# Moving token operands and weights of a hybrid decoder layer to eight different relative places within 512 bytes

## The chip, the cores and the metric

The kernel runs on one core of one Trainium2 chip. The metric is the device time of one execution in microseconds (us). A core has a matrix engine (TensorE, PE in the profile, with its weight loads as PEld), a vector engine (DVE), a scalar engine (ACT), GpSimd (POOL) and SyncE (SP), which here issues most DMAs. Operands of a matmul lie in SBUF, a memory of 128 partitions; a tile takes the same bytes in each partition, and "place" here means the byte address of a tile within a partition.

## The reference

One layer of a decoder on 512 tokens of width 2048, all in float32:

```
h = rmsnorm(x, attn_pre_norm)
proj = h @ w_in                      # 2048 x 6160: q, k, v, gate of 4 GLA heads,
                                     # 16 columns for the forget gate, q, k, v of 4 diff heads
o_a = rmsnorm(gla_chunked(q, k, v, log_sigmoid(ga @ w_alpha_up + b_alpha) / 16)) * silu(gate)
o_b = rmsnorm(diff_attention(q, k, v, lam)) * (1 - lambda_init)
x = x + rmsnorm(concat(o_a, o_b) @ w_o, attn_post_norm)
h = rmsnorm(x, ffn_pre_norm)
a, b = split(h @ w_ffn_in)           # 2048 x 11264, two branches of 5632
a = causal depthwise conv of width 3 over the tokens, with bias
f = (gelu(a) * b) @ w_ffn_out        # 5632 x 2048
x = x + rmsnorm(f, ffn_post_norm)
```

## The kernel before, in words

**Products in three parts.** Each float32 operand of a large product is held as a high part rounded to the matmul's own format (float32r) and a low part, the rest. A product is three matmuls into the same PSUM bank: high by high, and the two cross products. `split` (L127, L128) makes the parts of token operands: ACT writes the high part, DVE the low one by subtraction. `granule` (L104 to L117) does the same to a loaded piece of weights of 128 x 1024: `raw` becomes `whi` (L114, ACT) and `wlo` (L115, DVE), three buffers each; where a spare pool is given, the pieces are called `xhi` and `xlo`.

**Token operands.** `ah` and `al` hold the high and the low part of all 512 tokens by 2048 features, as 4 token blocks by 16 feature blocks of 128 x 128. They are rewritten three times: normed input, mixer output, input of the FFN, and in the down projection they hold the sums of the hidden values.

**Order.** The mixer's input projections come first: `proj_t` (products at L150 to L152: weights stationary, 512 tokens streamed) and `proj_n` (L168 to L170: tokens stationary, 512 weight columns streamed). Attention and gated linear attention are generators whose steps are filled in between projection steps. The forget gate (L364, L365) has its own small stationary weights, a tile `gas` of 16 groups of 80 columns in the pool `mx`. The output projection follows with the FFN's first pieces (`to_ffn`, an order written out by hand). All other stages are ordered by the planner, which simulates the engines and lets each instruction go where its operands and buffers would be ready.

**The FFN in units.** After a first group of 512 hidden columns the up projection runs in 20 units (10 groups by two branches). A unit computes a 2 x 2 block product with seven instead of eight block products (Strassen and Winograd's scheme), so it needs sums of token blocks: `s5`, `s2`, `s3` (and `s7`, which overwrites a block of `ah`, `al`). These sums are made once by `up_sums`, each as a high and a low tile of 8 KB per partition: `s5h`, `s5l`, `s2h`, `s2l`, `s3h`, `s3l`, in the pool `fa`. The products are L897 to L899: a 128 x 128 weight block is stationary, 256 token columns are streamed. `Unit.run` takes the segments in the order `a11`, `s5`, `s2`, `s3`, `a12`, `s7`, `a22`. POOL and SP load and add weight blocks.

At the end of each second unit `token_sums` makes four sums of the hidden values on DVE (L965), `s5`, `s2`, `s7`, `s3` in that order, each in a tile of tag `sum` with four buffers, and each is stored to DRAM by a DMA on SP's queue. `s2` reads `s5`, `s3` reads `s2`. The down projection (L994 to L996) runs in 10 units with the tokens stationary and 512 weight columns streamed, and reads the stored sums back.

**Where tiles lie.** Pools are stacked in the order in which they are opened; within a pool tiles follow each other. A pool that is closed gives its room to the next. Left to right: `pad` (128 bytes), `ah`, `al` (32768 bytes each), the pool `w` (`raw`, `whi`, `wlo`, 4096 bytes each), then the mixer's pools, of which the first (`mx1`) holds a tile `masks` of 1792 bytes; after the mixer the pool `wo` of the output projection; and after that `rp` (four `rt` of 4096 bytes) and `fa` (the six sums, six `u`, two `p1`, four `sum`). `masks` is the only tile among the matmul operands' pools whose length, modulo 512, isn't 0. `fa` ends where the pools on the right side begin, to the byte.

Of the kernel before, what the change touches and what calls it, by code (L numbers as in the profile page):

```python
# [9 lines left out]
F32 = mybir.dt.float32  # L10
F32R = mybir.dt.float32r
# [6 lines left out]
P = 128  # L18
# [17 lines left out]
def hybrid_layer(ctx: ExitStack, tc: tile.TileContext, x, attn_pre_norm, w_in, w_alpha_up, b_alpha,  # L36
# [3 lines left out]
    nc = tc.nc  # L40
# [6 lines left out]
    def dma(o, i):  # L47
        return nc.sync.dma_start(out=o, in_=i)
# [9 lines left out]
    const = ctx.enter_context(tc.tile_pool(name="const", bufs=1))  # L58
# [9 lines left out]
    nc.vector.memset(nhalf, -0.5)  # L68


    pad = const.tile([P, 32], F32, name="pad")
    nc.vector.memset(pad, 0.0)
    ah = const.tile([P, NT, KT, P], F32R, name="ah")
    al = const.tile([P, NT, KT, P], F32R, name="al")
    wpool = ctx.enter_context(tc.tile_pool(name="w", bufs=3))

    def bank(pool=None):
# [653 lines left out]
    fp = fa.enter_context(tc.tile_pool(name="fa", bufs=2))  # L731
# [43 lines left out]
    HK = KT // 2  # L775
    part = {"a11": (0, 0), "a12": (0, 1), "s7": (1, 0), "a22": (1, 1)}
    up = {}
    for n, (i, j) in part.items():
        up[n] = tuple(v[:, 2 * i:2 * i + 2, HK * j:HK * (j + 1), :] for v in (ah, al))
    for n in ("s5", "s2", "s3"):  # L780
        up[n] = tuple(fp.tile([P, 2, HK, P], F32R, name=f"{n}{v}", bufs=1) for v in "hl")
    s7raw = []

    def up_sums():
# [170 lines left out]
    def token_sums(gi, u0, u1):  # L955
        c, i = (gi - 1) // 2, (gi - 1) % 2
        T = [slice(0, 256), slice(256, 512)]
        a11, a21, a12, a22 = u0[:, :, T[0]], u0[:, :, T[1]], u1[:, :, T[0]], u1[:, :, T[1]]

        def put(n, src):  # L960
            dma(sd[c][n][:, i, :].rearrange("p (n t) -> p n t", n=2), src)

        def add(n, x, y, op):
            t = fp.tile([P, 2, 256], F32, name=n, tag="sum", bufs=4)
            tt(t, x, y, op)  # L965
            put(n, t)
            return t

        put("a11", a11)
        put("a12", a12)  # L970
        put("a22", a22)
        s5 = add("s5", a21, a22, ALU.subtract)
        s2 = add("s2", s5, a11, ALU.subtract)
        add("s7", a11, a21, ALU.subtract)
        add("s3", s2, a12, ALU.add)
# [219 lines left out]
```

## Time and profile before

| | |
|---|---|
| median of 3 runs | 2190.66 us (2188.64 to 2194.54) |
| profiled execution | 2189.8 us |
| its span, first to last instruction | 2188.1 us |
| mean granted TensorE clock | 0.996 |
| instructions | 31879, of which 13009 matmuls and as many weight loads |

Lines of groups read: line of the kernel, engine, operation, written tile <- read tiles, shapes, count, then busy time in us and mean ns of one, then idle time of the engine just before and what ended it. Lines of the timeline read: start in us, duration in us, engine, line, operation. The duration of a matmul reaches from its start to the end of its last column's way through the array and overlaps the next one's; the distance between starts is what a matmul costs in a dense stretch.

### The profile page before, as it was taken

The numbers are of one execution on the slowest core, as the hardware profiler recorded it, in microseconds if no ns is written. First come the engines' busy times: TensorE is split into PE (matmuls) and PEld (weight loads), VectorE is DVE, ScalarE is ACT, GpSimd is POOL, SyncE is SP. The second block draws the span as 40 slices with busy tenths as digits, with TensorE's granted clock in tenths as the row PEclk, the third lists the DMA queues.
The fourth block names the chain that finished last, engine by engine and source line by source line (L and its number), as shares of the span: only waits on it lengthen the run. The fifth ranks groups of instructions, "written<-read, shape, count | busy, mean of one in ns | idle before, by whom it ended". The sixth has DMA issues, their size and how long they took to land.

```text
span 2188.1 us, 31879 instructions
## 1 busy us (share of the span) xinstructions
PE 2152.7 (98%) x13009; PEld 1921.7 (88%) x13009; DVE 1418.9 (65%) x1722; ACT 901.2 (41%) x1162; POOL 204.6 (9%) x245
## 2 busy tenths in 40 slices
PE   7999999999999999999999999999999999999997
PEld 6878888888888889899999999999999878787886
DVE  5345554444453245886786776776777777888987
ACT  4233332333342233453443444444444464544433
POOL 1000000000000000011111111011011011011101
PEclk9999999999999999999999999999999999999999
DMA  6322222223224344447657667567567678677663
GB/s 210 103 68 79 76 78 77 78 77 87 78 87 166 104 154 154 124 109 179 154 126 183 145 136 181 138 150 175 134 157 178 173 212 218 173 187 184 151 175 136
DMA packets 218471, 303.83 MB, mean 139 GB/s; under 512 B 11776, under 2 KB 155572, under 8 KB 216404
## 3 DMA queue, kind: packets, MB, share of 16 engines
q1 hardware_dynamic: 165204, 238.87, 32.4%
q0 software_dynamic: 53120, 62.92, 18.5%
q8 instruction: 102, 1.67, 0.3%
q14 instruction: 45, 0.37, 0.0%
HBM read 273.97 MB, written 27.79 MB: 138 GB/s over the span
## 4 chain that ended last, share of the span: by engine, by line
issue 50%; PE 42%; POOL 4%; DVE 2%; DMA 1%; ACT 1%; POOLq 0%; SPq 0%; DVEq 0%; ACTq 0%
PE bank L168 7%; PE bank L169 7%; PE bank L170 7%; PE bank L152 5%; PE bank L150 5%; PE bank L151 4%; POOL rt L846 2%; POOL raw L846 2%; PE bank L417 1%; PE bank L995 1%; PE bank L996 1%; PE bank L994 1%; PE bank L485 1%; PE bank L516 1%; PE bank L135 1%
## 5 line engine op out<-in xcount | busy, mean ns | idle before, releaser
L115 DVE TENSOR_TENSOR wlo<-raw,whi 128x1024 fp32r<-128x1024 f32 x307 | 374.7, 1223 | 357.8 <-ACT whi L114 346.7
L114 ACT ACTIVATE whi<-raw 128x1024 fp32r<-128x1024 f32 x307 | 324.6, 1058 | 604.7 <-PE bank L898 185.6
L899 PE MATMUL bank<-ah,wlo 128*128 128x256 f32 x1280 | 362.9, 284 | 0.0
L898 PE MATMUL bank<-al,whi 128*128 128x256 f32 x1280 | 362.9, 284 | 0.0
L897 PE MATMUL bank<-ah,whi 128*128 128x256 f32 x1280 | 362.9, 284 | 0.0
L115 DVE TENSOR_TENSOR wlo<-rt,whi 128x1024 fp32r<-128x1024 f32 x220 | 268.1, 1222 | 114.9 <-ACT whi L114 114.6
L114 ACT ACTIVATE whi<-rt 128x1024 fp32r<-128x1024 f32 x220 | 232.1, 1058 | 260.9 <-PE bank L898 201.3
L897 PEld LDWEIGHTS bank<-ah,whi 128*128 128x128 f32 x1280 | 246.3, 192 | 0.1
L898 PEld LDWEIGHTS bank<-al,whi 128*128 128x128 f32 x1280 | 246.2, 192 | 0.1
L899 PEld LDWEIGHTS bank<-ah,wlo 128*128 128x128 f32 x1280 | 246.2, 192 | 0.0
L168 PE MATMUL bank<-whi,ah 128*128 128x512 f32 x600 | 237.5, 399 | 0.8 <-ACT ah L127 0.8
L169 PE MATMUL bank<-wlo,ah 128*128 128x512 f32 x600 | 236.3, 394 | 0.0
L170 PE MATMUL bank<-whi,al 128*128 128x512 f32 x600 | 235.5, 394 | 0.0
L150 PE MATMUL bank<-ah,whi 128*128 128x512 f32 (+1 forms) x512 | 196.4, 384 | 0.0
L152 PE MATMUL bank<-ah,wlo 128*128 128x512 f32 (+1 forms) x512 | 194.9, 381 | 0.0
L151 PE MATMUL bank<-al,whi 128*128 128x512 f32 (+1 forms) x512 | 194.8, 380 | 0.0
L995 PE MATMUL bank<-wlo,ah 128*128 128x512 f32 x420 | 164.1, 391 | 2.2 <-DVE wlo L115 2.2
L996 PE MATMUL bank<-whi,al 128*128 128x512 f32 x420 | 163.6, 390 | 0.0
L994 PE MATMUL bank<-whi,ah 128*128 128x512 f32 x420 | 156.4, 391 | 0.6 <-DVE acc L1002 0.6
L170 PEld LDWEIGHTS bank<-whi,al 128*128 128x128 f32 x600 | 113.4, 189 | 24.3 <-DVE al L128 0.3
L168 PEld LDWEIGHTS bank<-whi,ah 128*128 128x128 f32 x600 | 113.4, 189 | 24.1 <-ACT ah L127 1.2
L169 PEld LDWEIGHTS bank<-wlo,ah 128*128 128x128 f32 x600 | 113.5, 189 | 23.6 <-DVE wlo L115 0.5
(251 smaller groups left out, 4110.9 us busy)
## 6 DMA issues: line engine op xcount, KB each, us to landing
raw<-in_w_in_dram SPq DMA_DIRECT2D x96, 512.0 KB, 3.7
raw<-in_w_ffn_in_dram SPq DMA_DIRECT2D x96, 512.0 KB, 4.7
raw<-in_w_ffn_out_dram SPq DMA_DIRECT2D x48, 512.0 KB, 6.3
rt<-in_w_ffn_in_dram SPq DMA_DIRECT2D x40, 512.0 KB, 5.6
rt<-in_w_ffn_in_dram POOLq DMA_DIRECT2D x40, 512.0 KB, 5.9
raw<-in_w_ffn_in_dram POOLq DMA_DIRECT2D x40, 512.0 KB, 7.0
raw<-in_w_o_dram SPq DMA_DIRECT2D x32, 512.0 KB, 3.7
rt<-in_w_ffn_out_dram SPq DMA_DIRECT2D x20, 512.0 KB, 6.9
```

Source lines behind the costliest of these rows:

```text
L114: act(hi, raw, AF.Copy)
L115: tt(lo, raw, hi.bitcast(F32), ALU.subtract)
L150: mm(o, wh, ah[:, t0:t1, kk, :], start=st, stop=False)
L151: mm(o, wh, al[:, t0:t1, kk, :], start=False, stop=False)
L152: mm(o, wl, ah[:, t0:t1, kk, :], start=False, stop=sp)
L168: mm(banks[t], ah[:, t, s, :], w[0][:, k, :], start=st, stop=False)
L169: mm(banks[t], ah[:, t, s, :], w[1][:, k, :], start=False, stop=False)
L170: mm(banks[t], al[:, t, s, :], w[0][:, k, :], start=False, stop=sp)
L897: mm(o, wh, sh[:, :, kk, :], start=start and kk == 0 and n == 0, stop=False, **NOW)
L898: mm(o, wh, sl[:, :, kk, :], start=False, stop=False, **NOW)
L899: mm(o, wl, sh[:, :, kk, :], start=False, stop=kk == HK - 1, **NOW)
L995: mm(b[j], sh[:, o:o + P], w[1][:, q, :], start=False, stop=False, **NOW)
```

## The change

Nine small tiles that only take room ("rooms") are put between tiles that matmuls read, each filled once with zeros by DVE. Before and behind `al` stand rooms of 32 words (128 bytes), so that `ah`, `al` and the weight pool lie 128 bytes apart within 512 bytes; `room0` is the former `pad`. In the pool `fa` the six high and low tiles of the sums are allocated in another order, each behind a room of 8 to 48 words. The sums of the hidden values get three buffers in place of four, which makes the space for the rooms: `s3` then takes the buffer of `s5`. No matmul, conversion or DMA is added or removed.

Counted from the start of the weight pool within 512 bytes, the token tiles lie, after the change: `ah` at 256, `al` at 384, `s2l` at 192, `s2h` at 320, `s3l` at 352, `s5l` at 416, `s5h` at 480, `s3h` at 32. Before it all lie at 0. In the pool `wo` and in the pool of the down stage, which hold no rooms, spare weights lie as those of `w` do, before and after.

```diff
-    pad = const.tile([P, 32], F32, name="pad")
-    nc.vector.memset(pad, 0.0)
+    def room(pool, name, words):
+        nc.vector.memset(pool.tile([P, words], F32, name=name, bufs=1), 0.0)
+
+    room(const, "room0", 32)
     ah = const.tile([P, NT, KT, P], F32R, name="ah")
+    room(const, "room1", 32)
     al = const.tile([P, NT, KT, P], F32R, name="al")
+    room(const, "room2", 32)
     wpool = ctx.enter_context(tc.tile_pool(name="w", bufs=3))
...
+    late = {}
+    for n, words in (("s2l", 48), ("s2h", 32), ("s3l", 8), ("s5l", 16), ("s5h", 16), ("s3h", 16)):
+        room(fp, f"room{n}", words)
+        late[n] = fp.tile([P, 2, HK, P], F32R, name=n, bufs=1)
     for n in ("s5", "s2", "s3"):
-        up[n] = tuple(fp.tile([P, 2, HK, P], F32R, name=f"{n}{v}", bufs=1) for v in "hl")
+        up[n] = (late[n + "h"], late[n + "l"])
...
         def add(n, x, y, op):
-            t = fp.tile([P, 2, 256], F32, name=n, tag="sum", bufs=4)
+            t = fp.tile([P, 2, 256], F32, name=n, tag="sum", bufs=3)
             tt(t, x, y, op)
```

## The prediction

> **What bounds the kernel now.** I read the page's busy shares and its slices first, then the table of windows, then PE's timeline, then the weight loads and who waits for whom.
>
> ```profile
> PE 2152.7 (98%) x13009; PEld 1921.7 (88%) x13009; DVE 1418.9 (65%) x1722; ACT 901.2 (41%) x1162; POOL 204.6 (9%) x245
> PE   7999999999999999999999999999999999999997
> PEclk9999999999999999999999999999999999999999
> ```
>
> TensorE is busy in 98% of the span, in every slice but the first and the last at 90% or more, and its clock is granted throughout. So the time is the number of matmuls times the distance between their starts. That distance is what the change can touch, and it has to be read from starts, since the durations in the page overlap.
>
> ```profile
> 75.00:380.00 305.00, 305.00 (x1474) 254.86 (x1474) 147.38 (x243) 98.42 (x148) 16.65 (x32) 1.00 0.26 78
> 932.00:1740.00 808.00, 808.00 (x6713) 806.88 (x6711) 594.45 (x601) 372.74 (x405) 102.49 (x80) 1.00 0.65 154
> ```
>
> Columns: the stretch, its length, then busy time and count of PE, PEld, DVE, ACT, POOL, clock, DMA share, GB/s. The second stretch is the up projection by units: 808.00 us over 6713 matmuls of 256 columns are 120.4 ns each, with weight loads going on nearly all the time (806.88 us) and no hole in PE. In the first stretch PE has no hole either. The long matmuls stand in the timeline; here are the first and the last of 58 in a row (57 distances):
>
> ```profile
> 492.45 0.39 PE L152 MATMUL bank<-ah,wlo 128*128 128x512 f32 x1
> ...
> 505.37 0.39 PE L152 MATMUL bank<-ah,wlo 128*128 128x512 f32 x1
> ```
>
> (505.37 - 492.45) / 57 = 226.7 ns for 512 columns. From 256 to 512 columns the distance grows by 106.3 ns, so 226.7 is twice that plus 14, and 120.4 is that plus 14: each matmul carries some 14 ns beside its columns, in both shapes. A part of it comes from the weight load that runs beside it:
>
> ```profile
> 844.27 0.19 PEld L150 LDWEIGHTS bank<-ah,xhi 128*128 128x128 f32 x1
> 844.39 0.19 PEld L151 LDWEIGHTS bank<-al,xhi 128*128 128x128 f32 x1
> 845.14 0.19 PEld L152 LDWEIGHTS bank<-ah,xlo 128*128 128x128 f32 x1 [0.55 <-DVE xlo L115]
> 845.25 0.19 PEld L150 LDWEIGHTS bank<-ah,xhi 128*128 128x128 f32 x1
> 845.37 0.19 PEld L151 LDWEIGHTS bank<-al,xhi 128*128 128x128 f32 x1
> ```
>
> Beside a running matmul loads start 0.12 us apart (844.27 to 844.39, and 845.25 to 845.37). After the wait, with no matmul streaming, the next load starts 0.11 us later (845.14 to 845.25). So about 10 ns of the 120 go with the reading of weights and of the streamed operand at the same time. In before all these operands lie at the same place within 512 bytes: every tile between `ah` and the `fa` pool is a multiple of 512 bytes long.
>
> **The change, part by part.** *Places.* After the change the weights lie, counted from the token operand within 512 bytes, at 256 (`ah`), 128 (`al`), 320 (`s2l`), 192 (`s2h`), 160 (`s3l`), 96 (`s5l`), 32 (`s5h`), 480 (`s3h`); in before at 0 for all. Where tokens are the stationary operand (output projections, down units) 256 stays and 128 turns into 384. What runs beside matmul n is the weight load of matmul n+1, so one triple (high by high, and the two cross products) has two pairs at the relation of its high part and one at that of its low part. No instruction is added to TensorE. The counts, from the groups with shapes kept apart (the three products of a triple have equal counts):
>
> ```profile
> L899 PE MATMUL bank<-ah,wlo 128*128 128x256 f32 x1280 | 362.9, 284 | 0.0
> L168 PE MATMUL bank<-whi,ah 128*128 128x512 f32 x600 | 237.5, 399 | 0.8 <-ACT ah L127 0.8
> L150 PE MATMUL bank<-ah,whi 128*128 128x512 f32 x448 | 178.2, 398 | 0.0
> L995 PE MATMUL bank<-wlo,ah 128*128 128x512 f32 x420 | 164.1, 391 | 2.2 <-DVE wlo L115 2.2
> L899 PE MATMUL bank<-s3h,wlo 128*128 128x256 f32 x320 | 90.7, 284 | 0.0
> L995 PE MATMUL bank<-xlo,ah 128*128 128x512 f32 x140 | 55.9, 399 | 0.6 <-DVE xlo L115 0.4
> L1102 PE MATMUL bank<-wlo,ah 128*128 128x512 f32 x56 | 21.9, 391 | 0.2 <-DVE wlo L115 0.2
> ```
>
> What does another relation cost? Before has two places that show one. The first granule of spare weights in the opening stage (`xhi`, `xlo` of pool `mx`) lies 256 from `ah` and `al`, since `masks` is 1792 bytes long:
>
> ```profile
> 51.85 0.40 PE L169 MATMUL bank<-xlo,ah 128*128 128x512 f32 x1
> 52.09 0.39 PE L170 MATMUL bank<-xhi,al 128*128 128x512 f32 x1
> 52.32 0.39 PE L168 MATMUL bank<-xhi,ah 128*128 128x512 f32 x1
> ...
> 52.99 0.39 PE L170 MATMUL bank<-whi,al 128*128 128x512 f32 x1
> ```
>
> After two slow ones behind the transposes (0.24, 0.23), three distances take 0.67 us, 223 ns each with the rounding of the rows, which is not above the 226.7. So relation 256 costs nothing, and that covers all pairs whose high part is `ah`. The other place is the forget gate, whose weights `gas` advance by 320 bytes per step, and so pass through 256, 64, 384, 192, 0, 320, 128 and 448 while `ah` and `al` stream:
>
> ```profile
> 124.47 0.40 PE L364 MATMUL bank<-ah,gas 128*80 128x512 f32 x1
> 124.71 0.39 PE L365 MATMUL bank<-al,gas 128*80 128x512 f32 x1
> 124.94 0.39 PE L364 MATMUL bank<-ah,gas 128*80 128x512 f32 x1
> 125.17 0.39 PE L365 MATMUL bank<-al,gas 128*80 128x512 f32 x1
> ...
> 131.58 0.39 PE L365 MATMUL bank<-al,gas 128*80 128x512 f32 x1
> 131.81 0.39 PE L168 MATMUL bank<-whi,ah 128*128 128x512 f32 x1
> ```
>
> 32 distances take 131.81 - 124.47 = 7.34 us, 229.4 ns each, 2.7 ns above the 226.7 at relation 0; the largest is 0.24 us, about 13 ns above. These loads have 80 columns rather than 128, and their relation changes every second matmul, as the relation in the changed kernel does within each triple. I take the mean, +2.7 ns, for each pair at a relation other than 0 and 256, in both shapes, because the 14 ns were the same in both:
>
> - 512 columns: the rows give 600 + 448 + 420 + 140 + 56 = 1664 triples, one pair each at 128 or 384: 1664 x 2.7 ns = 4.5 us.
> - 256 columns on `ah`/`al`: 1280 x 2.7 ns = 3.5 us.
> - 256 columns on the six late tiles: 3 operands x 3 products x 320 = 2880 matmuls, all moved: 2880 x 2.7 ns = 7.8 us.
>
> Together 15.8 us, all of it on the path, since PE has no holes there. Both ends of the price: below, the 10 ns of the load beside a matmul vanish for the moved pairs of 256 columns, (1280 + 2880) x 10 ns = -42 us (the long ones have the load in the first half of the stream, where I see no gain). Above, every moved pair costs the gate's largest, (1664 + 1280 + 2880) x 13 ns = +76 us. The mean lies between them and comes from the nearest rows, so I take it.
>
> *The rooms.* Nine fills on DVE in place of one, by the one that is there:
>
> ```profile
> L72 DVE MEMSET pad<- 128x32 f32 x1 | 0.1, 85 | 0.0
> PE bank L168 <- ACT ah L127: 0.8, 1, 0.8
> PE bank L995 <- DVE wlo L115: 2.2, 5, 0.5
> ```
>
> 85 ns each: 8 x 0.085 = 0.7 us. Two more at the start lie where DVE waits for the first inputs. The six late ones go over memory that the output projection used, so DVE has to wait until its last reader, PE on the spare weights among them, is done, and the conversions of the next weights queue behind. Three weight buffers cover that; the longest that PE waits for a converted `wlo` in the whole run is 0.5 us. I cost it at nothing, and if that cover is gone, at a few us once: 0 to +5. A gain isn't possible, as nothing is taken away.
>
> *One buffer fewer for the sums.* `s3` now takes the buffer of `s5`, whose store must have landed:
>
> ```profile
> 1020.13 0.69 DVE L965 TENSOR_TENSOR s<-u 128x512 f32<-128x512 f32 x1
> ...
> 1025.94 0.69 DVE L965 TENSOR_TENSOR s<-s,u 128x512 f32<-128x512 f32 x1
> 1020.85 6.13 SPq L48 DMA_DIRECT2D sd0s<-s  x4
> sd3s<-s SPq DMA_DIRECT2D x8, 256.0 KB, 3.8
> ```
>
> `s5` ends at 1020.82 and its store is issued at 1020.85 on SP's queue; the slowest group of these stores takes 3.8 us in the median, so it lands near 1024.7, and `s3` starts at 1025.94: 1.2 us to spare. Should a store be late by 2 us, DVE would stand still with the next `wlo` behind it, ten times in the run. DVE is busy 594 of 808 us there and has holes to make it up, so 0, at most 10 x 2 = +20 us if PE had to wait each time. The planner may also order DVE's work a little differently; with PE's waits as small as above I take 0.
>
> **The sum.** The profiled execution took 2189.8 us (span 2188.1 and 1.7 around it). 2189.8 + 15.8 = 2205.6; it stands 0.9 us below the median of the runs, 2190.66, so I forecast 2206 us, 0.7% slower. A change within 0.3%, some 6.6 us, is about what a measurement of this kernel can't tell from none.
>
> **The rivals.** *Nothing happens* (2190 us): the 14 ns are a fixed price per matmul, and places don't enter. For it: the row at relation 256, and that 226.7 and 120.4 carry the same extra. Against it: the gate's matmuls, at 229.4 with a shorter load. The Trainium skill says the same in "SBUF — State Buffer", section "Who interferes with whom": PE has two independent read ports, one for the streamed operand and one for weights; "TensorE: Matmul & The Clock Gate", section "Step-by-step: what each phase is for", adds that loading the next weights takes no read bandwidth from the running matmul. By that rule the time would stay 2190.7; this trace agrees only in part, since loads beside a matmul go 0.12 us apart and 0.11 without.
>
> *The collision is freed* (faster): if the 10 ns exist because both reads are at the same place within 512 bytes, moving them apart ends it. Place: the up units, where loads run back to back. Price: the -42 us above, 2148 us. It decides from about 2.7 ns per moved pair of 256 columns: 4160 x 2.7 = 11.2 us pays for the 4.5 us of the long ones and leaves 0.3%. For it: the first short matmul behind a long one,
>
> ```profile
> 927.91 0.28 PE L897 MATMUL bank<-ah,whi 128*128 128x256 f32 x1
> 928.02 0.28 PE L898 MATMUL bank<-al,whi 128*128 128x256 f32 x1
> 928.14 0.28 PE L899 MATMUL bank<-ah,wlo 128*128 128x256 f32 x1
> ```
>
> takes 0.11, and the next 0.12 for the rest of the stage: the shape can go faster at some position of the two reads. Against it: relation 256 brings nothing to the long ones.
>
> *The collision gets heavy*: relations under 128 make one read follow the other, and every moved pair pays the gate's 13 ns: +76 us, 2266 us. For it: the gate's slowest distances come again and again. Against it: its mean is only 2.7.
>
> **How the numbers follow.** Chances: the forecast, a few ns per moved pair (2198 to 2230), 0.47; nothing, 0.13; freed, 0.28; heavy, 0.12. Faster by over 0.3% is the freed case, 0.28; within it 0.13; slower 0.47 + 0.12 = 0.59. The time is that of the likeliest case, 2206. The range takes in the freed case to 2150 and the heavy one to 2255, which leaves out the ends of both, some 0.1 on each side taken generously.
>
> **What would show it.** In the window of the up units, the length over the count: 120.4 now, about 121.5 if I am right (pairs on `ah` unchanged, the late tiles near 123), under 118 if freed, over 125 if heavy. In the long stages 226.7 to about 227.6. Within the up units the operands should differ from one another: the same distance for `s2`, `s3`, `s5` and `ah` would refute a dependence on place. DVE before `s3` should show no wait for a store, and PE's waits should stay below some us. Wrong would I be above all if 80-column loads say nothing on 128-column ones, for the price comes from them.

## The result, and the profile after

The changed kernel takes 2192.31 us (median of 10 runs), the kernel before 2192.10 us in the runs beside it: a ratio of 1.0005 with a 95% interval of 0.9995 to 1.0014. Nothing that a measurement can tell from no change, where 2206 us was forecast. Yet a great deal moved inside, in both directions.

The page of the changed kernel, its first lines:

```profile
span 2189.1 us, 31896 instructions
PE 2154.7 (98%) x13009; PEld 1909.7 (87%) x13009; DVE 1419.6 (65%) x1730; ACT 902.0 (41%) x1162; POOL 204.8 (9%) x245
```

TensorE's matmuls are as many as before, and it is as busy. The table of windows (the stretch, its length, busy time and count of PE, PEld, DVE, ACT, POOL, clock, DMA share, GB/s) separates the two shapes; the second stretch, 950 to 1650 us, lies inside the up units in every kernel of this study. First the kernel before, then the changed one:

```profile
950.00:1650.00 700.00, 700.00 (x5836) 700.00 (x5835) 511.64 (x520) 321.49 (x350) 89.83 (x70) 1.00 0.65 154
```

```profile
75.00:380.00 305.00, 305.00 (x1457) 251.85 (x1457) 146.91 (x242) 98.11 (x147) 16.22 (x32) 1.00 0.27 77
950.00:1650.00 700.00, 700.00 (x5940) 700.00 (x5939) 522.24 (x530) 326.98 (x355) 92.40 (x72) 1.00 0.66 155
```

In the up units 5940 matmuls fit where 5836 did: 117.8 ns each instead of 119.9. Between 75 and 380 us, where long matmuls prevail, only 1457 fit where 1474 did. The long ones in the timeline of the changed kernel, from the output projection; from the first row to the last are 131 distances:

```profile
689.69 0.39 PE L172 MATMUL bank<-whi,ah 128*128 128x512 f32 x1
689.92 0.40 PE L173 MATMUL bank<-wlo,ah 128*128 128x512 f32 x1
690.15 0.40 PE L174 MATMUL bank<-whi,al 128*128 128x512 f32 x1
...
719.98 0.40 PE L174 MATMUL bank<-whi,al 128*128 128x512 f32 x1
```

30.29 / 131 = 231.2 ns, against 226.7 before. The starts in the trace tell the three products of a triple apart, which the rounded rows don't: in this stretch it is 227.0 ns on average from the first product to the second, 232.4 from the second to the third, and 234.3 from the third to the next first, where the kernel before has 226 to 227 for each. The operands of the up units differ as well: from 116.8 ns behind a product with `s2l` to 120.1 ns behind one of `s5h` with `wlo`, where before all stand at 120.0.

What the stages make of it shows in the first and the last matmul of the up units in the changed kernel:

```profile
940.21 0.28 PE L905 MATMUL bank<-ah,whi 128*128 128x256 f32 x1
...
1737.95 0.28 PE L907 MATMUL bank<-ah,wlo 128*128 128x256 f32 x1
```

and the last one in the kernel before, whose first stands at 927.91 in the prediction:

```profile
1739.64 0.28 PE L899 MATMUL bank<-ah,wlo 128*128 128x256 f32 x1
```

The units begin 12.3 us later (long matmuls ahead of them), take 797.7 instead of 811.7 us, 14.0 less, and from their last matmul to the end of the span it is 451.2 instead of 448.5 us, 2.7 more. Together +1.0 us, the difference of the spans. Two real effects cancel.

### The profile page after: what moved, and what is told of

It is laid out like the page before. It is cut to its first block, busy times and chain, and to the rows that moved or that the text cites. A ratio compares the mean times of both kernels' runs of the same rounds, so it can differ in the third digit from the quotient of the medians.

```text
span 2189.1 us, 31896 instructions
## 1 busy us (share of the span) xinstructions
PE 2154.7 (98%) x13009; PEld 1909.7 (87%) x13009; DVE 1419.6 (65%) x1730; ACT 902.0 (41%) x1162; POOL 204.8 (9%) x245
## 4 chain that ended last, share of the span: by engine, by line
PE 77%; issue 17%; DVE 2%; DMA 1%; POOL 1%; ACT 1%; SPq 0%; POOLq 0%; DVEq 0%; ACTq 0%
PE bank L173 6%; PE bank L174 6%; PE bank L906 6%; PE bank L907 6%; PE bank L905 6%; PE bank L172 6%; PE bank L1003 6%; PE bank L1004 6%; PE bank L154 5%; PE bank L156 5%; PE bank L1002 5%; PE bank L155 5%; PE bank L421 1%; PE bank L489 1%; PE bank L520 1%
## 5 line engine op out<-in xcount | busy, mean ns | idle before, releaser
L907 PE MATMUL bank<-ah,wlo 128*128 128x256 f32 x1280 | 358.4, 280 | 0.0
L907 PEld LDWEIGHTS bank<-ah,wlo 128*128 128x128 f32 x1280 | 241.8, 189 | 0.0
L905 PEld LDWEIGHTS bank<-ah,whi 128*128 128x128 f32 x1280 | 240.8, 188 | 0.1
L906 PEld LDWEIGHTS bank<-al,whi 128*128 128x128 f32 x1280 | 240.3, 188 | 0.1
L173 PE MATMUL bank<-wlo,ah 128*128 128x512 f32 x600 | 238.9, 399 | 0.0
L174 PE MATMUL bank<-whi,al 128*128 128x512 f32 x600 | 238.7, 400 | 0.0
L1003 PE MATMUL bank<-wlo,ah 128*128 128x512 f32 x420 | 166.3, 396 | 0.4 <-DVE wlo L119 0.4
L1004 PE MATMUL bank<-whi,al 128*128 128x512 f32 x420 | 166.5, 397 | 0.0
```

The source lines that it names most:

```text
L173: mm(banks[t], ah[:, t, s, :], w[1][:, k, :], start=False, stop=False)
L174: mm(banks[t], al[:, t, s, :], w[0][:, k, :], start=False, stop=sp)
L905: mm(o, wh, sh[:, :, kk, :], start=start and kk == 0 and n == 0, stop=False, **NOW)
L906: mm(o, wh, sl[:, :, kk, :], start=False, stop=False, **NOW)
L907: mm(o, wl, sh[:, :, kk, :], start=False, stop=kk == HK - 1, **NOW)
L1004: mm(b[j], sl[:, o:o + P], w[0][:, q, :], start=False, stop=st == 3, **NOW)
```

## The experiments

**The two halves of the change.** Theory P: the place of weights relative to tokens sets the distance of matmul starts, and in opposite ways for the two shapes. Rival O: the planner ordered the work otherwise and time only moved between stages. Each half of the change alone tells them apart. The rooms in the pool `fa` alone:

```diff
     ah = const.tile([P, NT, KT, P], F32R, name="ah")
-    room(const, "room1", 32)
     al = const.tile([P, NT, KT, P], F32R, name="al")
-    room(const, "room2", 32)
```

> Theory P (the place sets the distance of starts, in opposite ways for the two shapes): the trace of the changed kernel shows the 256-column matmuls of the late tiles at 116.8 to 120.1 ns, mean 118.2, where before had 120.0, and the 512-column ones at 227 to 234 where before had 227. With the rooms in the pool fa alone, the 512-column ones go back to 227, ah and al in the up units to 120.0, and the late tiles stay near 118.2: 2880 x 1.8 ns = 5 us less than before, 2187 us. Rival O (the planner's other order moved time between the stages; places cost nothing): the same time as before, 2192 us, and late tiles at any value that changes with the order.

Measured: 2185.28 us against 2189.77, ratio 0.998 (0.9971 to 0.9989): 4.5 us less. The windows:

```profile
75.00:380.00 305.00, 305.00 (x1471) 254.16 (x1472) 147.33 (x243) 98.12 (x147) 16.67 (x32) 1.00 0.27 79
950.00:1650.00 700.00, 700.00 (x5875) 700.00 (x5874) 514.46 (x521) 322.78 (x352) 89.85 (x70) 1.00 0.66 155
```

The long stretch is back (1471, before 1474); the units keep a part of the gain, 119.1 ns. By operand, from the starts in the trace, `ah` and `al` are at 120.0 ns again and the late tiles at 118.2, both as expected.

The rooms around `al` alone:

```diff
     for n, words in (("s2l", 48), ("s2h", 32), ("s3l", 8), ("s5l", 16), ("s5h", 16), ("s3h", 16)):
-        room(fp, f"room{n}", words)
         late[n] = fp.tile([P, 2, HK, P], F32R, name=n, bufs=1)
```

> The rooms at ah and al alone. Theory P: the up units begin about 12 us later than in before (928 us), as in the changed kernel; ah and al in the units at 117.7 ns, the late tiles back at 120 ns; in sum 6 us more than before, 2198 us. Rival O: 2192 us.

Measured: 2196.63 us, ratio 1.003 (1.0018 to 1.0041): 6.9 us more. The windows:

```profile
75.00:380.00 305.00, 305.00 (x1456) 251.88 (x1456) 146.88 (x242) 98.17 (x147) 16.38 (x32) 1.00 0.26 77
950.00:1650.00 700.00, 700.00 (x5901) 700.00 (x5901) 518.40 (x526) 325.62 (x354) 91.11 (x71) 1.00 0.65 154
```

The long stretch is as slow as in the changed kernel (1456), and the units keep the gain of `ah` and `al`, 118.6 ns: `ah` and `al` are at 117.8 ns there, the late tiles at 119.8. The two halves, -4.5 and +6.9 us, make +2.4, which agrees with the change's +0.05% within the intervals. Rival O expected no change of either, and falls.

**The lost buffer.** Only `bufs=3` for the sums, in the kernel before:

> No room added, only three buffers for the sums of the hidden values. Both theories: the same time as before within 0.1%, 2192 us; DVE doesn't wait for a store. If it is slower, the lost buffer hid a gain of the places in the changed kernel.

Measured: 2188.84 us, ratio 1.0001 (0.9992 to 1.0011). It costs nothing. In the changed kernel DVE waited once, 0.8 us, for a store:

```profile
DVE s L973 <- DMA sd4s<-s: 0.8, 1, 0.8
```

**All places in one kernel.** To take the alternation within a triple away, the weights were moved and the tokens left: each up unit, down unit and projection reads its weights at one place.

```diff
-            hi = wpool.tile([P, GR], F32R, name="whi", tag="whi")
+            hi = wpool.tile([P, GR + 128], F32R, name="whi", tag="whi")[:, at:at + GR]
...
-        return Unit(4, block, up_prods, chain, out)
+        return Unit(4, block, up_prods, chain, out, 8 * ((2 * (gi - 1) + br) % 16))
```

> Weights moved, tokens not: each up unit reads its weights at its own place, 0 to 480 bytes in steps of 32 from the tokens' (the same for high and low parts), each down unit and each projection at one of several. Space for it comes from two instead of four buffers of sums and from scratch tiles, so the time says nothing. Theory P: distances differ from unit to unit, 256-column ones between 112 and 122 ns with 120 at relation 0, 512-column ones 227 at 0 and up to 235. Rival A (not the relation itself counts but that it alternates within a triple): at a uniform relation all units show 120 and all long ones 227, whatever the relation.

The times of this kernel and of the finer scan below (2201.86 and 2193.22 us, one run each) say nothing, since their buffers are others. The distances differ from unit to unit although the relation is uniform, so rival A falls as the sole cause. Two stretches of 48 matmuls on `s5` in the timeline (47 distances each), first at 64 bytes in the third unit:

```profile
1029.93 0.28 PE L904 MATMUL bank<-s5h,whi 128*128 128x256 f32 x1
...
1035.46 0.28 PE L906 MATMUL bank<-s5h,wlo 128*128 128x256 f32 x1
...
1348.96 0.28 PE L904 MATMUL bank<-s5h,whi 128*128 128x256 f32 x1
...
1354.29 0.28 PE L906 MATMUL bank<-s5h,wlo 128*128 128x256 f32 x1
```

The first stretch gives 117.7 ns, the second, at 320 bytes, 113.4. The means by place, all stretches, from the starts in the trace (distances of 250 ns and more left out; ns):

| weights minus tokens, bytes | 256 columns, tokens streamed | 512 columns, tokens streamed | 512 columns, weights streamed |
|---|---|---|---|
| 0 / 256 | 120.4 / 120.0 | 226.7 / 228.8 | 228.0 / 228.3 |
| 32 / 288 | 118.3 / 118.3 | 233.3 / 233.1 | 233.3 / 233.3 |
| 64 / 320 | 115.3 / 113.4 | 233.2 / 233.3 | 229.5 / 229.5 |
| 96 / 352 | 119.6 / 119.8 | 234.1 / 234.0 | 233.6 / 233.3 |
| 128 / 384 | 119.6 / 119.6 | 232.3 / 232.3 | 233.0 / 232.7 |
| 160 / 416 | 120.0 / 120.0 | 233.3 / 233.4 | 234.1 / 234.2 |
| 192 / 448 | 117.8 / 117.8 | 229.4 / not set | 233.3 / 233.2 |
| 224 / 480 | 117.8 / 117.8 | 233.3 / not set | 233.1 / 233.4 |

Three readings. The pattern repeats after 256 bytes, not 512. The long matmuls are fastest where before has them, at 0 and 256; nearly everywhere else they lose 3% (only 192 with tokens streamed and 64 with weights streamed lose as little as 1%). The short ones are at their slowest at 0 and 256 and from 96 to 160, within 1 ns of one another, and gain 5% at best near 64. Within 64 itself the mean of 115.3 hides two values, 117.8 in the third unit and 113.3 in the nineteenth.

**Finer places.** The same with steps of mostly 4 bytes:

> As the scan before it, with finer places: up units at 8 to 120 bytes in steps of mostly 4, and some at 184 to 232; long matmuls at 0 to 24 and 232 to 272 bytes. Theory P with a period of 256 bytes: 113 ns near 64 with a width of some 16 to 32 bytes, the long ones at 227 near 0 and 256 and rising towards 233 within 32 bytes. A rival by which only whole steps of 32 bytes matter: equal distances within each 32 bytes. The time says nothing.

The expectation of a valley some 16 to 32 bytes wide was wrong. 256 columns: 117.8 at 44 and 48 bytes, 113.4 at 52, 117.8 at 56, 119.5 at 60, 114.0 at 64, 118.4 at 68, 118.3 at 72, 113.4 at 76, 118.8 at 80, 120.0 at 84, 113.5 at 88: from 52 to 88 low every 12 bytes, that is every third column of 4 bytes. At 40, one such step below 52, it was 119.2, and at 96, where the first scan had 120.0 in the steady stretches, it was 117.4. The long ones rise at once: with tokens streamed 226.7 at 0, 232.4 at 4; with weights streamed 227.7 at 0, 237.1 at 4. Equal distances within 32 bytes, the rival, are excluded too.

**The up units at 64 bytes, all else at 0 or 256.** Each weight buffer is 256 bytes longer, and the up units alone read 64 bytes further on; two scratch tiles of the mixer share a place to make room.

```diff
-            hi = wpool.tile([P, GR], F32R, name="whi", tag="whi")
-            lo = wpool.tile([P, GR], F32R, name="wlo", tag="wlo")
+            hi = wpool.tile([P, GR + 64], F32R, name="whi", tag="whi")[:, at:at + GR]
+            lo = wpool.tile([P, GR + 64], F32R, name="wlo", tag="wlo")[:, at:at + GR]
...
-        return Unit(4, block, up_prods, chain, out)
+        return Unit(4, block, up_prods, chain, out, 16)
```

> Weights 64 bytes beyond the tokens' place in the up units alone, at 0 or 256 everywhere else (each weight buffer takes 256 bytes more; three buffers of sums, and two scratch tiles share a place, to make room). Theory P: 6720 matmuls at 113.3 to 117.8 ns instead of 120.0, the long ones unchanged: 15 to 45 us less than before, 2145 to 2175 us. Rival A (only alternation counts): 2190 us.

Measured: 2175.72 us, ratio 0.9925 (0.9911 to 0.9938), just above the expected range. The window of the units:

```profile
950.00:1650.00 700.00, 700.00 (x5946) 700.00 (x5945) 521.51 (x528) 326.98 (x356) 89.84 (x70) 1.00 0.66 157
```

117.7 ns: the units sit in the slower of the two distances that 64 bytes showed in the scan, for the whole stage. No start in the stage comes late before 1713 us.

**52, 76 and 88 bytes.** One number is changed: 16 words become 13, 19 or 22.

> As the run with 64 bytes, but 52. At 64 the stage has two steady distances, 113.3 and 117.8 ns, and the run before stayed in the second from 931 us on; at 52 the fine scan showed only the first (113.4 in three stretches). Theory P with one steady distance at 52: 6720 x 6.6 ns = 44 us less than before, about 2147 us. Rival (what decides is how a stretch is entered, not the place): 117.8 again, 2175 us.

Measured: 2187.38 us, ratio 0.9987 (0.9971 to 1.0002), from 2174.8 to 2191.68 in single runs. Two stretches of its timeline, 85 and 90 distances long, in one execution:

```profile
1199.75 0.28 PE L899 MATMUL bank<-ah,whi 128*128 128x256 f32 x1
...
1209.95 0.28 PE L900 MATMUL bank<-al,whi 128*128 128x256 f32 x1
...
1459.79 0.28 PE L900 MATMUL bank<-s5l,whi 128*128 128x256 f32 x1
...
1469.99 0.28 PE L900 MATMUL bank<-s3l,whi 128*128 128x256 f32 x1
```

10.20 us for 85, 120.0 ns, and 10.20 us for 90, 113.3 ns, at the same place. In this execution the units ran at 120.0 until about 1444 us, at 113.3 until about 1596, and at 120.0 again. Both changes come with a late start; the first:

```profile
1443.95 0.28 PE L900 MATMUL bank<-al,whi 128*128 128x256 f32 x1
1444.13 0.38 PE L901 MATMUL bank<-ah,wlo 128*128 128x256 f32 x1
1444.35 0.28 PE L899 MATMUL bank<-ah,whi 128*128 128x256 f32 x1
```

Here 0.18 and 0.22 us stand in place of 0.12; the second change follows a distance of 0.83 us. So the place alone doesn't fix the distance: it allows several steady ones, and in the traces of the runs at 52, 64, 76 and 88 bytes the stage keeps its own until a start comes late.

> The same at 76 bytes, where the fine scan showed 113.4 too: 2147 us; by the rival 2175 us.

Measured: 2149.05 us, ratio 0.9816 (0.9804 to 0.9829), 2146.58 to 2150.55 in single runs. The windows:

```profile
75.00:380.00 305.00, 305.00 (x1475) 254.58 (x1475) 147.51 (x245) 98.51 (x148) 16.66 (x32) 1.00 0.26 78
950.00:1650.00 700.00, 699.06 (x6161) 698.39 (x6160) 537.66 (x547) 335.15 (x368) 95.11 (x74) 1.00 0.68 163
```

6161 matmuls in 700 us, 113.6 ns, and the long stretch as in before. Here each of the seven late starts between 930 and 1680 us (distances of 0.14 to 0.78 us) led back to 113.3. This version beats both kernels, by 1.8%.

> The same at 88 bytes, 113.5 in the fine scan: 2147 us; by the rival 2175 us.

Measured: 2163.36 us, ratio 0.9869 (0.9841 to 0.9897), single runs from 2147.97 to 2166.98: in its profiled execution most of the stage ran at 116.7 ns and some 115 us near its end at 113.3, and a late start stands at both changes (0.39 us at 941 us, 0.13 at 1586). At 52 and 88 the rival of this expectation was nearer to the truth: how a stretch is entered does count.

## Why the prediction was wrong

The bound was read rightly: the time is the count of matmuls times the distance of their starts, and places change that distance. Its sum failed in one step, "I take the mean, +2.7 ns, for each pair at a relation other than 0 and 256, in both shapes, because the 14 ns were the same in both".

- *256 columns.* The forecast added 3.5 + 7.8 us; the units lost 14.0 us. The equal 14 ns were no finding: they come from one line drawn through two points, 120.4 and 226.7, and such a line gives both shapes the same extra whatever the two distances are. The scan shows the shapes apart: at relation 0 the short ones were near their slowest and the long ones at their fastest. The freed case had the right sign for these, with 2.1 ns instead of its 10, and its sign in the sum was undone by the long ones.
- *512 columns.* The forecast added 4.5 us: in each triple one pair at +2.7 ns, and nothing for the two at 256. Measured with the tokens stationary are +0, +6 and +7 ns (227.0, 232.4 and 234.3 above), some 13 ns for a triple: the pair at 384 cost twice its price, and of the two at 256 the one ahead of it cost nothing and the one behind it 7 ns. With the tokens streamed all three rose, to 232.4, 233.0 and 229.9 from about 228. The row at relation 256 was right where all three products lie there (228 in the scan); within a triple that alternates it wasn't, so the relation of a pair alone doesn't give its cost. This made 12.3 us ahead of the units. Behind them 1848 distances, 4.2 ns longer in the mean, make 7.8 us; the stage lost only 2.7 because PE waited less there: 19 distances of 250 ns and more in place of 39, which are 4.8 us less waiting. Why it waited less, these runs don't tell.
- *The price itself.* The 2.7 ns came from loads of 80 columns at eight places. Over the places of the scan long ones lose 1 to 7 ns, so the mean was in the right region and its spread was missed. The row was also misread. By the starts in the trace the gate's largest distance is 237 ns, 10 above 226.7 and not 13, which came from rows rounded to 10 ns; and it comes back, at 236 to 237, with every eighth distance, always beside a load at 256 or at 0, the places that the prediction took as free. Eight distances are four steps of 320 bytes, together 256 modulo 512: the period of 256 bytes stood there already.
- *The rooms and the buffer.* Costed at nothing, and nothing is what they cost: a ratio of 1.0001 (0.9992 to 1.0011) for the buffer alone, with a single wait of DVE of 0.8 us in the changed kernel; and for the rooms, the distances of 250 ns and more ahead of the units sum to 64.2 us in both kernels.
- *The rivals.* "Nothing happens" gave the right time for a wrong reason: the distances did change, and only their sum didn't; that it hit the time was luck. Of the signs that the prediction named, the operands of the units did come to differ, the long stages rose to more than its 227.6, and the units fell from 119.9 to 117.8 ns in the window from 950 to 1650 us, about its sign for the freed case, under 118 (over the whole stage, as its 120.4 was read, it is 797.7 us over 6745 matmuls, 118.3): each half was foreseen as a sign, but not both together. "Heavy" didn't come: no place of the scans had a mean for the short ones above that of relation 0, and the long ones came nearest to its 13 ns with 237.1 at 4 bytes. The Trainium skill states in "SBUF — State Buffer", section "Who interferes with whom", that PE's two read ports are independent. What the prediction drew from it, that places don't enter, doesn't hold in these traces: with the same matmuls, and the weights of the up units 76 bytes further on, 6161 instead of 5836 fit into 700 us. Whether it is the ports that get in each other's way isn't shown.

## What to carry to other kernels

When two operands are streamed and loaded at the same time, their relative place in a partition is a parameter to be measured, by shape: one kernel that gives each stretch its own place measures a dozen of them at once. A time that doesn't move can be two effects that cancel, so do the halves alone before calling a change neutral. Two shapes give a slope and an extra, but no proof that the extra is the same in both; that takes a third shape. And take a gain that depends on such a place only after several runs: at 52 bytes the same program ran at 113 and at 120 ns.

## What the runs showed of the hardware

For float32r matmuls with a new 128-column weight load each, the distance of starts depends on the place of the weights relative to the tokens, with a period of 256 bytes, and down to steps of 4 bytes: 113.3 to 120.4 ns for 256 columns, 226.7 to 237.1 ns for 512, as means of a place. Moving the tokens alone (rooms in `fa`) and moving the weights alone (the scans) both do it; a run that moves both by the same amount, to set the relative place against the absolute one, is missing. The two shapes don't share their best place (0 or 256 for the long ones, 76 for the short ones here). For 256 columns a place can hold more than one steady distance: 113.3 and 117.8 at 64, 113.3 and 120.0 at 52, 113.3 and 116.7 at 88; within the stage at one place a change came with a late start. What makes these, and why the low ones come every 12 bytes, these runs don't tell: the collision of the two reads was argued from the 0.11 and 0.12 us between loads, not shown. The 0.11 us were to hold with no matmul streaming, but the trace of before has a matmul that starts together with that load:

```profile
845.14 0.39 PE L152 MATMUL bank<-ah,xlo 128*128 128x256 f32 x1 [0.35 <-DVE xlo L115]
```
